# Writing out SyncE's order from branch a on, and moving branch a's gate sigmoids behind each panel's evacuation

## The chip, the core and the metric

The kernel runs on one core of a Trainium2 chip. The core has TensorE (PE; its weight loads are listed apart as PEld), VectorE (DVE), ScalarE (ACT), GpSimd (POOL) and SyncE (SP), which here issues most of the DMAs. Each engine works through its own queue in order; semaphores make one wait for another. The metric is the device time of one execution in microseconds, lower is better.

## The reference

One layer of a hybrid encoder on 1024 prompt rows and 64 sample rows (1088 in all, kept transposed, channels on partitions):

```python
z = xn @ w_in                                  # one wide projection
xa, ga, q, k, v, gb, fl, ma, mb = jnp.split(z, ...)
...                                            # branch a: conv, recurrence; branch b: attention
ya = ya * jax.nn.silu(ga)
yb = yb.reshape(B, L, W_B) * jax.nn.silu(gb)
u = jnp.einsum('bsnw,nwd->bsnd', jnp.stack([ya, yb], axis=2), w_branch)
gates = jax.nn.sigmoid(jnp.stack([ma, mb], axis=2))
mix = jnp.sum(gates * u, axis=2) @ w_o
h = x + rms_norm(mix, g_post)
...
```

The change lies in the lines from `u` to `mix`: sigmoid(ma) * (ya @ w_branch[0]) + sigmoid(mb) * (yb @ w_branch[1]), and the beginning of `@ w_o`.

## The kernel before

All products are float32 in effect, made of three matmuls: each operand is split into a high part (`copy_act`, line 84, on ACT) and a low part (`sub`, line 87, on DVE or POOL), and PE adds high by high (L166), low by high (L167) and high by low (L168).

**Branch a** computes ya @ w_branch[0] in eight panels of 128 output channels (`of` 0 to 7), each of 72 matmuls: 8 input blocks, three column chunks of 368, 368 and 352, three matmuls. Panels 0 and 1 are mostly computed earlier and only finished here (`finish_held`). A panel's raw weights come from DRAM in pairs of panels (`load_panel`, four DMAs of 256 KB on SP, L248); `panel()` takes the next panel, splits the weights of the one behind it (`wh` on ACT, `wl` on DVE) and starts loads when buffers are free. `evac_a` (L1976) multiplies each chunk in PSUM by the gate into a buffer `s`, of which there are two, and L1978 stores it to `d_mix` in DRAM. The gates come as two halves of 544 columns: `half_gate` (L1918) loads one from `d_ma`, `open_gate` (L1922) takes its sigmoid on ACT; there are five such buffers. In panels 3 to 6 `branch_b` also makes the operands of branch b: on POOL yb times its gate, on ACT the high parts `b`, on DVE the low parts and the sums `t`.

**Branch b** computes yb @ w_branch[1] by Strassen's scheme in the form with seven products for two by two blocks: four iterations `i`, each with seven products of 24 matmuls (`product_b`, L2095), on operands `b`, `t0` to `t9` (each split into `t..h` and `t..l` by `split_t`). `put_b` finishes one half panel: two operations on DVE (sum, times the gate), one on POOL (plus branch a's half, `ma_in`, loaded back from `d_mix`), and a store to `d_mx` (L2110). `load_b` fetches the weights of a later iteration. `next_g` and `next_m` issue the loads of the next gate and the next `ma_in`. In the last iteration the raw weights of w_o are loaded (`load_w`, L2056), and `mix_room` (L2082) loads finished panels of `d_mx` back, which `split_mix` splits into `mxh` and `mxl`.

**w_o** starts when branch b's last product is issued: its first 4 input blocks need `wo[0, 0]` and `mix` 0 to 3, the others `wo[0, 1]` (`wqh`, `wql`) and `mix` 4 to 7.

**Order.** A scheduler orders each engine's queue, except within `tc.manual_schedule(engines=...)`: there the named engines keep the order in which the code is written. From branch a's finish to `split_mix(4, 5, 6, 7)` this holds for ACT, DVE and POOL; PE is ordered by the scheduler in both kernels. The panel loads on SP are pinned in program order one by one (`tc.keep_in_program_order`); the rest of SP is the scheduler's.

Of the kernel before, what the change touches and what calls it, by code (L numbers as in the profile page):

```python
# [15 lines left out]
KT = D // P  # L16
# [51 lines left out]
def hybrid_step(tc, a, o):  # L68
# [171 lines left out]
    held_back = [True]  # L240
    n_single = [0]
    ahead = deque()

    def load_panel(dst, src, pin=lambda inst: inst):

        n = KT // 4
        for i in range(4):
            pin(sp.dma_start(dst[:, i * n:(i + 1) * n, :], src[i * n * P:(i + 1) * n * P].rearrange(  # L248
                "(k p) n -> p k n", p=P)))

    def look_ahead():

        while len(ahead) < 2:
            if held_back[0] and len(gates) <= n_gates - PLAIN // 2:
                return
            if not (gates or later):
                return
            src, tags = (gates or later)[0]
            if any(not e[3] and max(len(tags), e[4]) > 1 for e in ahead):
                return  # L260
            (gates or later).popleft()
            if len(tags) > 1:
                dst = raw_pair
                raws_ = panels(raw_pair)
            else:
                dst = raw_half[n_single[0] % 2].rearrange("p (k n) -> p k n", k=KT)
                raws_ = [dst]
                n_single[0] += 1
            load_panel(dst, src, tc.keep_in_program_order)
            for tag, raw in zip(tags, raws_):  # L270
                ahead.append([tag if isinstance(tag, tuple) else ("r", tag), raw, None, False, len(tags)])

# [8 lines left out]
    def panel(eng=None):  # L281

        look_ahead()
        if not ahead:
            return None
        split_next(eng or dve)
        tag, _, w, *_ = ahead.popleft()
        look_ahead()
        split_next(eng or dve)
        look_ahead()  # L290
        return tag, w
# [634 lines left out]
    w = first_w  # L926
    for i in range(len(quads)):
# [10 lines left out]
        w = w_nxt  # L938
# [897 lines left out]
    def finish_held(i, evac):  # L1836
        wh, wl = takes[i][0]["w"]
        for (c, (t0, n)), acc in zip(enumerate(CH), accs["a", i]):
            k = KT - 1
            three(acc[:, :n], wh[:, k, :], wl[:, k, :], ya[k][0][:, t0:t0 + n], ya[k][1][:, t0:t0 + n], False, True)  # L1840
            evac(c, t0, n, acc[:, :n])
# [74 lines left out]
    def half_gate(src, h):  # L1916
        g = p5.tile([P, HT], F32, name="gate", tag="gate", bufs=5)
        sp.dma_start(g[:, :], src[:, H[h]])  # L1918
        return g

    def open_gate(g):
        act.activation(out=g[:, :], in_=g[:, :], func=AF.Sigmoid)  # L1922
        return g

    def gate_in(of):
        return [open_gate(half_gate(d_ma[of], h)) for h in range(2)]

    seq = tc.manual_schedule(engines={act.engine, dve.engine, pool.engine})
    seq.__enter__()
    look_ahead()  # L1930
    split_next(dve, spare)
    fetch(0)
# [30 lines left out]

    w_b = [{} for _ in range(5)]
    g_next = gate_in(0)
    for of in range(KT):
        g = g_next
        if of + 1 < KT:
            g_next = gate_in(of + 1)

        def evac_a(c, t0, n, z, s=None):
            s = s or p5.tile([P, HT], F32, name="s", tag="s", bufs=2)
            for h in range(2):
                a_, b_ = max(t0, h * HT), min(t0 + n, (h + 1) * HT)
                if a_ < b_:
                    dve.tensor_tensor(out=s[:, a_ - t0:b_ - t0], in0=z[:, a_ - t0:b_ - t0],  # L1976
                                      in1=g[h][:, a_ - h * HT:b_ - h * HT], op=ALU.mult)
            sp.dma_start(d_mix[of][:, t0:t0 + n], s[:, :n])  # L1978

        if of < 2:  # L1980
            finish_held(of, evac_a)
        else:
            tag, w = panel()
            assert tag == ("a", of)
            if 3 <= of < 7:
                branch_b(of - 3)
            if of == KT - 2:
                p4.close()
                sp_ = sb("quad_b")
                load_b(0)  # L1990
                splits = split_pair(0, panels(b_raw[0]), w_b[0])
            if of < KT - 1:
                run(panel_steps(mm, *w, ya, evac_a))
            else:
                for _ in range(3):
                    next_g()
                next(splits)
                next(splits)
                wh, wl = w
                mm.close()  # L2000
                psq = ps("psq_b", bufs=4)
                two = [psq.tile([P, 2, 512], F32, name="quad_b") for _ in range(2)]
                accs_ = [two[0][:, 0, :], two[0][:, 1, :], two[1][:, 0, :]]
                ks = (3, 4, 0, 7, 6, 5, 1, 2)
                for k in ks:
                    for c, (t0, n) in enumerate(CH):
                        three(accs_[c][:, :n], wh[:, k, :], wl[:, k, :], ya[k][0][:, t0:t0 + n], ya[k][1][:, t0:t0 + n],
                              k == ks[0], k == ks[-1])
        if of == 2:
            ft_p = mm.tile([P, 512], F32, name="ft_p", tag="acc")  # L2010
            pe.transpose(ft_p[:64, :P], fin.rearrange("p s k -> p (s k)"), ident[:, :])
            ft = p5.tile([P, HT], F32, name="s", tag="s", bufs=2)[:64, :P]
            dve.tensor_copy(ft, ft_p[:64, :P])
            at = 0
            for name, n in (("conv_prompt", 24), ("conv_sample", 24), ("h_prompt", 8), ("h_sample", 8)):
                sp.dma_start(o[name], ft[at:at + n, :])
                at += n
# [83 lines left out]
    def put_b(of, h, z, in1):  # L2101

        g, m = g_got.popleft(), m_got.popleft()
        n_out[0] += 1
        s = (p5.tile([P, HT], F32, name="s", tag="s", bufs=2) if n_out[0] % 3 else late.tile([P, HT], F32, name="s_"))
        s3 = s.rearrange("p (c n) -> p c n", c=2)
        dve.tensor_tensor(out=s3, in0=z, in1=in1, op=ALU.add)
        dve.tensor_tensor(out=s[:, :], in0=s[:, :], in1=g[:, :], op=ALU.mult)
        pool.tensor_tensor(out=s[:, :], in0=s[:, :], in1=m[:, :], op=ALU.add)
        sp.dma_start(d_mx[of][:, H[h]], s[:, :])  # L2110
        next_g()
        next_m()
        open_next()

    def bank():
# [8 lines left out]
    for i in range(4):  # L2124
        w, first, last = w_b[i], i == 0, i == 3
        d1, d2 = 2 * i, 2 * i + 1
        own, splits = splits, iter(()) if last else split_pair(i + 1, panels(b_raw[i + 1]), w_b[i + 1])

        def more():
            next(splits, None)  # L2130

        ta, za = bank()
        product_b(ta, w["a11"], B11, True)
        p1_ = part("p1_")
        copy_act(p1_, za)
        if last:
            raws_ = [load_w(a["w_o"], 0, 0, j) for j in range(2)]
            mix_room(0, "b0", "b2")
            mix_room(1, "b1", "b3")
        td, zd = bank()  # L2140
        product_b(td, w["a12"], B21, True)
        put_b(d1, 0, zd, p1_)
        more()
        if first:
            split_t(8)
            split_t(9)
        else:
            more()
        if last:
            wo[0, 0] = split_w(raws_[0], *small_room())  # L2150
            mix_room(2, "b4", "b6")
            mix_room(3, "b5", "b7")
        elif i + 2 < 4:
            load_b(i + 2)
        tb, zb = bank()
        product_b(tb, w["s2"], T2, True)
        u2 = part("u2_")
        dve.tensor_tensor(out=u2, in0=zb, in1=p1_, op=ALU.add)
        if first:
            next(own)  # L2160
        elif last:
            split_mix(0, 1)
        tcc, zc = bank()
        product_b(tcc, w["s1"], T1, True)
        product_b(tb, w["s3"], T3, False)
        u3 = part("u3_")
        dve.tensor_tensor(out=u3, in0=zb, in1=p1_, op=ALU.add)
        put_b(d2, 1, zc, u3)
        more()
        if last:  # L2170
            split_mix(2, 3)
            mix_room(4, "t0", "t1")
            mix_room(5, "t2", "t3")
        te, ze = bank()
        product_b(te, w["a22"], T4, True)
        put_b(d2, 0, ze, u3)
        more()
        if first:
            more()
        if last:  # L2180
            wo[0, 0] += split_w(raws_[1], *small_room())
        product_b(tcc, w["s4"], B22, False)
        put_b(d1, 1, zc, u2)
        more()
# [289 lines left out]
```

## Time and profile before

| | |
|---|---|
| median of 3 runs | 1443.7 us (1441.4 to 1445.7) |
| profiled execution | 1445.49 us, span on the core 1443.4 us |
| TensorE's granted clock, mean | 0.992 of full speed |
| PE busy | 1409.9 us, 98% of the span |
| DVE, ACT, POOL busy | 910.8, 727.7, 354.7 us |
| moved by DMA | 191.63 MB, mean 133 GB/s |

All times are from the start of the span. Busy times are of an engine; what stands in brackets behind a row is how long the engine had been idle before it and what ended that wait. Branch a's panels 0 to 2 end at 1039.5 us, panel 7 ends at 1113.9, branch b's last product ends at 1206.95, and w_o's first use of `wo[0, 1]` is at 1224.47.

### The profile page before, as it was taken

How to read it: one execution, taken by the hardware profiler on the slowest of the kernel's cores; microseconds unless marked ns; L12 is line 12 of the kernel's file. 1: busy time of each engine (PE TensorE's matmuls, PEld its weight loads, DVE VectorE, ACT ScalarE, POOL GpSimd, SP SyncE). 2: the span in 40 equal slices, each digit the busy share in tenths (PEclk: the TensorE clock that was granted, in tenths of full speed). 3: DMA queues.
4: the chain of work that ended last, by engine and by line, in shares of the span. 5: the costliest groups of instructions: out<-in, count | busy, mean ns of one | idle time of the engine just before them, and what ended most of it. 6: DMA issues, size and time to landing. Idle time of an engine off the chain costs nothing.

```text
span 1443.4 us, 24408 instructions
## 1 busy us (share of the span) xinstructions
PE 1409.9 (98%) x9063; PEld 1335.1 (93%) x9063; DVE 910.8 (63%) x1558; ACT 727.7 (50%) x1338; POOL 354.7 (25%) x430
## 2 busy tenths in 40 slices
PE   9999999999999999999999999999898899999997
PEld 9999999999999999999999899999898898787886
DVE  6646665665662576676766668798456866338544
ACT  5415344344341666666666667878214334324533
POOL 0002332322311444333343400000244454000000
PEclk9999999999999999999999999999999999999999
DMA  5376555655427767556655533421676667224111
GB/s 207 116 131 110 109 176 167 187 169 158 97 74 207 199 142 145 141 136 137 152 137 126 66 67 41 67 41 48 213 233 197 191 200 280 80 73 148 48 47 45
DMA packets 140466, 191.63 MB, mean 133 GB/s; under 512 B 22980, under 2 KB 97772, under 8 KB 140348
## 3 DMA queue, kind: packets, MB, share of 16 engines
q1 hardware_dynamic: 121500, 156.57, 44.1%
q10 hardware_dynamic: 16240, 23.97, 4.6%
q0 software_dynamic: 2608, 9.54, 2.0%
q8 instruction: 71, 1.16, 0.4%
q14 instruction: 47, 0.39, 0.1%
HBM read 127.11 MB, written 62.92 MB: 132 GB/s over the span
## 4 chain that ended last, share of the span: by engine, by line
PE 86%; DMA 5%; DVE 4%; issue 2%; ACT 2%; SPq 1%; DVEq 0%; ACTq 0%; POOL 0%; POOLq 0%
PE quad L810 19%; PE acc L166 12%; PE acc L167 12%; PE acc L168 12%; PE quad_b L2095 5%; PE tp L1193 4%; PE s L1168 2%; PE s L1167 2%; PE pv L1222 2%; PE pv L1220 2%; DMA gate<-d_ma 2%; PE vacc L166 1%; DMA w_raw<-in_w_in 1%; PE vacc L167 1%; PE vacc L168 1%
## 5 line engine op out<-in xcount | busy, mean ns | idle before, releaser
L166 PE MATMUL acc<-xh,wh 128*128 128x368 f32 (+1 forms) x672 | 227.5, 339 | 0.4
L167 PE MATMUL acc<-xl,wh 128*128 128x368 f32 (+1 forms) x672 | 219.8, 327 | 0.0
L168 PE MATMUL acc<-xh,wl 128*128 128x368 f32 (+1 forms) x672 | 219.5, 327 | 0.0
L166 PEld LDWEIGHTS acc<-xh,wh 128*128 128x128 f32 x672 | 126.4, 188 | 1.9 <-DVE nm L1147 1.3
L167 PEld LDWEIGHTS acc<-xl,wh 128*128 128x128 f32 x672 | 126.7, 189 | 0.6
L168 PEld LDWEIGHTS acc<-xh,wl 128*128 128x128 f32 x672 | 126.4, 188 | 0.0
L87 DVE TENSOR_TENSOR wl<-w_raw,wh 128x1024 fp32r<-128x1024 f32 (+1 forms) x67 | 76.8, 1148 | 74.8 <-ACT wh L84 73.1
L84 ACT ACTIVATE th<-tp 128x512 fp32r<-128x512 f32 (+1 forms) x160 | 86.8, 550 | 64.5 <-PE tp L1193 54.1
L87 DVE TENSOR_TENSOR tl<-tp,th 128x512 fp32r<-128x512 f32 (+1 forms) x160 | 99.2, 634 | 29.4 <-ACT th L84 27.8
L1153 POOL TENSOR_SCALAR pb<-pb,sm 128x640 f32<-128x640 f32 (+1 forms) x64 | 61.8, 965 | 166.2 <-DVE sm L1152 155.3
L84 ACT ACTIVATE wh<-w_raw 128x1024 fp32r<-128x1024 f32 (+1 forms) x67 | 62.5, 936 | 76.4 <-PE quad L810 42.7
L810 PE MATMUL quad<-xh,wh 128*128 128x272 f32 x448 | 93.9, 291 | 0.0
L810 PE MATMUL quad<-xl,wh 128*128 128x272 f32 x448 | 92.6, 288 | 0.0
L810 PE MATMUL quad<-xh,wl 128*128 128x272 f32 x448 | 92.5, 288 | 0.0
L84 ACT ACTIVATE wh<-s 128x512 fp32r<-128x512 f32 x54 | 34.1, 631 | 84.0 <-PE quad L810 48.3
L1150 ACT ACTIVATE pb<-pb,nm 128x640 f32<-128x640 f32 (+1 forms) x64 | 63.3, 989 | 24.8 <-DVE nm L1147 17.2
L1220 PE MATMUL pv<-tl,vv 128*128 128x512 f32 x192 | 70.0, 365 | 2.1 <-DVE y L1232 1.3
L810 PEld LDWEIGHTS quad<-xl,wh 128*128 128x128 f32 x448 | 70.6, 188 | 0.0
L810 PEld LDWEIGHTS quad<-xh,wl 128*128 128x128 f32 x448 | 70.4, 188 | 0.0
L810 PEld LDWEIGHTS quad<-xh,wh 128*128 128x128 f32 x448 | 70.2, 188 | 0.2
L1167 PE MATMUL s<-k,q 128*128 128x128 f32 (+2 forms) x192 | 67.4, 358 | 0.0
L1147 DVE CUSTOM_DVE_ANT_0 pb<-s,mask 128x640 f32<-128x640 f32 (+1 forms) x64 | 64.8, 1012 | 3.7 <-PE s L1168 3.5
(702 smaller groups left out, 3958.4 us busy)
## 6 DMA issues: line engine op xcount, KB each, us to landing
w_raw<-in_w_in SPq DMA_DIRECT2D x56, 256.0 KB
q<-d_q SPq DMA_DIRECT2D x48, 256.0 KB
k<-d_k SPq DMA_DIRECT2D x48, 256.0 KB
w_raw<-in_w_in SPq DMA_DIRECT2D x56, 128.0 KB
wraw<-in_w_in SPq DMA_DIRECT2D x24, 256.0 KB
w_raw<-in_w_branch SPq DMA_DIRECT2D x24, 256.0 KB
d_k<-oh ACTq DMA_DIRECT2D x16, 272.0 KB
d_k<-kl SPq DMA_DIRECT2D x16, 272.0 KB
```

The lines of the kernel that those rows point to most:

```text
L84: return act.activation(out=out, in_=in_, func=AF.Copy, scale=scale)
L87: return eng.tensor_tensor(out=out, in0=in0, in1=in1, op=ALU.subtract)
L166: pe.matmul(out, ah, bh, start=start, stop=False)
L167: pe.matmul(out, ah, bl, start=False, stop=False)
L168: pe.matmul(out, al, bh, start=False, stop=stop)
L810: pe.matmul(acc[:, c, :CW], l[:, k, :], r[:, k, c * CW:(c + 1) * CW], start=(first and k == 0 and p == 0), stop=(k == 3 and p == 2), skip_ ...
L1147: at = book("D", now[0] + HOP_PE, per(D_MAX, n), lambda: dve.tensor_tensor_reduce(out=pr[:, :n], in0=s[:, :n], in1=m, scale=-1.0, scalar=- ...
L1150: at = book("A", at, per(A_EXP, n), lambda: act.activation(out=pr[:, :n], in_=pr[:, :n], func=AF.Exp, scale=-1.0, bias=nm, accum_out=sm))
L1153: return free, book("G", at, per(G_NORM, n), lambda: pool.tensor_scalar(out=pr[:, :n], in0=pr[:, :n], scalar1=sm, scalar2=1.0, op0=ALU.mul ...
L1167: pe.matmul(s[:, c0:c0 + w], t["q1"][:, q], t["k1"][:, c0:c0 + w], start=True, stop=False)
L1220: pe.matmul(pv[:, 512 - n:], v, tl[:, c:c + n], start=(j == 0), stop=False)
L2095: pe.matmul(acc[:, c, :CW], l[:, k, :], r[k // 2][:, k % 2, c * CW:(c + 1) * CW], start=(first and k == 0 and p == 0), stop=(k == 3 and p ...
```

## The change

It does five things, all within the region whose order is written out:

1. SP joins the engines whose order is written; the pins on the panel loads are dropped from there on (`pinned.clear()`).
2. `gate_in` only loads; the sigmoids of panel `of + 1` are taken behind the evacuation of panel `of`.
3. In panel 1 (`of == 1`), `panel()` is called ahead of the evacuations instead of in panel 2.
4. In `put_b` the loads of the next gate and the next `ma_in` are written ahead of the store (the first call leaves them out).
5. `load_b(i + 2)` stands behind the iteration's second `put_b` instead of its first.

```diff
+    pinned = [tc.keep_in_program_order]
...
-            load_panel(dst, src, tc.keep_in_program_order)
+            load_panel(dst, src, *pinned)
...
     def gate_in(of):
-        return [open_gate(half_gate(d_ma[of], h)) for h in range(2)]
-
-    seq = tc.manual_schedule(engines={act.engine, dve.engine, pool.engine})
+        return [half_gate(d_ma[of], h) for h in range(2)]
+
+    seq = tc.manual_schedule(engines={act.engine, dve.engine, pool.engine, sp.engine})
     seq.__enter__()
+    pinned.clear()
...
     g_next = gate_in(0)
+    for g in g_next:
+        open_gate(g)
...
-        if of < 2:
+        if of == 0:
             finish_held(of, evac_a)
+        elif of == 1:
+            left_over = []
+            finish_held(of, lambda *args: left_over.append(args))
+            tag, w = panel()
+            for args in left_over:
+                evac_a(*args)
         else:
-            tag, w = panel()
+            if of > 2:
+                tag, w = panel()
...
+        if of + 1 < KT:
+            for g_ in g_next:
+                open_gate(g_)
...
         g, m = g_got.popleft(), m_got.popleft()
+        if n_out[0]:
+            next_g()
+            next_m()
         n_out[0] += 1
...
         sp.dma_start(d_mx[of][:, H[h]], s[:, :])
-        next_g()
-        next_m()
         open_next()
...
-        elif i + 2 < 4:
-            load_b(i + 2)
...
         put_b(d2, 1, zc, u3)
         more()
+        if i + 2 < 4:
+            load_b(i + 2)
```

What it moves, in the order of the queues. On ACT, from the beginning of branch a's finish (`gate` is a sigmoid, `wh` the split of a panel's weights, `b` a split of branch b's operands), before:

```order
L1922 ACTIVATE gate<-gate 128x544 x8
L84 ACTIVATE wh<-w_raw 128x1024
L1922 ACTIVATE gate<-gate 128x544 x2
L84 ACTIVATE wh<-w_raw 128x1024
L84 ACTIVATE b_12543<-yb_in 128x544
L84 ACTIVATE b_12545<-yb_in 128x544
L1922 ACTIVATE gate<-gate 128x544 x2
```

and now:

```order
L1923 ACTIVATE gate<-gate 128x544 x4
L84 ACTIVATE wh<-w_raw 128x1024
L1923 ACTIVATE gate<-gate 128x544 x4
L84 ACTIVATE wh<-w_raw 128x1024
L84 ACTIVATE b_12541<-yb_in 128x544
L84 ACTIVATE b_12543<-yb_in 128x544
```

The split of panel 3's weights had eight sigmoids ahead of it and has four, that of panel 4 had ten and has eight: each later split has two sigmoids (one panel) fewer ahead of it.

On SP at the same place (`gate<-d_ma` a half gate's load, `d_mix<-s` a chunk's store, `w_raw<-in_w_branch` the load of a pair of panels, here 4 and 5), before:

```order
L1918 DMA gate<-d_ma 128x544 x5
L1978 DMA d_mix<-s 128x368
L1918 DMA gate<-d_ma 128x544
L1978 DMA d_mix<-s 128x368
L1978 DMA d_mix<-s 128x352
L1918 DMA gate<-d_ma 128x544
L1978 DMA d_mix<-s 128x368
L1918 DMA gate<-d_ma 128x544
L1978 DMA d_mix<-s 128x368
L1978 DMA d_mix<-s 128x352
L1918 DMA gate<-d_ma 128x544
L248 DMA w_raw<-in_w_branch 128x2x256 x4
```

and now:

```order
L1919 DMA gate<-d_ma 128x544 x4
L1982 DMA d_mix<-s 128x368 x2
L1982 DMA d_mix<-s 128x352
L1919 DMA gate<-d_ma 128x544 x2
L249 DMA w_raw<-in_w_branch 128x2x256 x4
L1982 DMA d_mix<-s 128x368 x2
L1982 DMA d_mix<-s 128x352
```

A panel's three stores stand together and its two gate loads behind them, and the load of the pair stands behind panel 0's stores instead of panel 1's.

On SP at the end of branch b (`d_mx<-s` a half panel's store, `mxl<-d_mx` a finished panel's load, `w_raw<-in_w_o` half of a block of w_o), before:

```order
L2110 DMA d_mx<-s__14127 128x544
L2056 DMA w_raw<-in_w_o 128x2x512
L2110 DMA d_mx<-s 128x544
L2082 DMA mxl_14170<-d_mx 128x1088
L2056 DMA w_raw<-in_w_o 128x2x512
L2082 DMA mxl_14167<-d_mx 128x1088
```

and now:

```order
L2127 DMA d_mx<-s__14127 128x544
L2224 DMA g_post<-in_g_post 128x1024
L2127 DMA d_mx<-s 128x544
L2096 DMA mxl_14167<-d_mx 128x1088
L2096 DMA mxl_14170<-d_mx 128x1088
L2070 DMA w_raw<-in_w_o 128x2x512 x2
```

The two loads for `wo[0, 1]` now stand together, behind the last store and behind the loads of panels 6 and 7. Those for `wo[0, 0]`, which had stood among the stores of the third iteration, likewise stand together now behind the twelfth store (`d_mx<-s__13914`).

## Prediction

> **What bounds the kernel now.** I read the busy table first, then one window for each stage, then the waits of each engine in the stages that the edit touches, then the chain and the timelines. From the page:
>
> ```profile
> span 1443.4 us, 24408 instructions
> PE 1409.9 (98%) x9063; PEld 1335.1 (93%) x9063; DVE 910.8 (63%) x1558; ACT 727.7 (50%) x1338; POOL 354.7 (25%) x430
> ```
>
> TensorE is the bound; only 1443.4 − 1409.9 = 33.5 us of the span can be won without removing a matmul. The windows show how much of it lies here (span of the stage, then busy time of PE, PEld, DVE, ACT, POOL, then PE's granted clock). They are panels 3 to 7 of branch a, and branch b:
>
> ```profile
> 1039.50:1113.90 74.40, 64.35 (x363) 62.33 (x361) 40.83 (x50) 21.10 (x29) 31.71 (x29) 0.93 0.65 206
> 1113.90:1207.00 93.10, 87.70 (x675) 87.09 (x674) 69.32 (x78) 38.28 (x56) 46.05 (x27) 0.96 0.67 220
> ```
>
> PE is idle there for 10.1 and 5.4 us, and both stages have a clock under 1. What they could take is read from PE's timeline: panel 7 runs without a wait, and so does the last product of branch b (12 pairs at 0.25).
>
> ```profile
> 1101.96 0.33 PE L166 MATMUL quad_b<-yah,wh 128*128 128x368 f32 x1
> ...
> 1113.92 0.66 PE L2095 MATMUL quad_b<-b,wh 128*128 128x272 f32 x4
> ...
> 1206.20 0.41 PE L2095 MATMUL quad_b<-t9h,wh 128*128 128x272 f32 x2
> 1206.45 0.41 PE L2095 MATMUL quad_b<-t9l,wh 128*128 128x272 f32 x2
> ```
>
> A panel is 11.96 us, a product 3.0. So panels 3 to 7 lose 74.4 − 5 × 11.96 = 14.6 us, and branch b (28 products) loses 93.1 − 84.0 = 9.1: together 23.7 us. The waits of PE, ACT and DVE in these stages say on whom:
>
> ```profile
> PE acc L166 <- ACT wh L84: 8.3, 2, 4.8
> PE quad_b L2095 <- DVE u__13275 L2158: 3.0, 1, 3.0
> PE quad_b L2095 <- DVE s L1976: 2.4, 1, 2.4
> ACT gate L1922 <- DMA gate<-d_ma: 55.9, 8, 14.5
> DVE s L1976 <- DMA d_mix<-s: 27.5, 9, 6.0
> ```
>
> PE waits 8.3 us for a weight split on ACT, and ACT has stood 55.9 us in front of gate sigmoids whose loads had not landed. The chain of waits shows how the two hang together:
>
> ```profile
> 1077.14 0.99 DVE s L1976 x3
> 1078.13 7.78 DMA gate<-d_ma
> ...
> 1086.57 1.05 ACT wh L84
> ...
> 1095.01 0.96 DVE s L1976 x3
> 1095.98 3.21 DMA gate<-d_ma
> ...
> 1100.94 1.24 DVE wl L87
> ```
>
> It is a ring: DVE's evacuation frees a gate buffer, the next gate half loads into it, its sigmoid stands on ACT ahead of wh, then come wl and branch b's pieces on DVE, and behind these the next evacuation. One turn takes 13 to 18 us (from wl at 1069.77, below, to 1087.6 and 1100.94), and PE wants one every 11.96.
>
> **The change, part by part.**
>
> *Sigmoids behind the evacuation, gate loads in pairs.* No instruction is added or removed. The wh split no longer has the sigmoids that depend on the last evacuation ahead of it, but those of one panel earlier, so the DMA link (7.78, 3.21) leaves the ring. What is late next is DVE itself. Its rows (start, duration, idle before):
>
> ```profile
> 1069.77 1.23 DVE L87 TENSOR_TENSOR wl<-w_raw,wh 128x1024 fp32r<-128x1024 f32 x1 [5.21 <-ACT wh L84]
> ...
> 1073.57 3.65 DVE L87 TENSOR_TENSOR t<-yb_in,t 128x544 f32<-128x544 f32 x1
> 1077.14 1.04 DVE L1976 TENSOR_TENSOR s<-acc,gate 128x368 f32<-128x368 f32 x3
> 1083.64 0.52 DVE L1976 TENSOR_TENSOR s<-acc,gate 128x352 f32<-128x352 f32 x1 [5.47 <-DMA d_mix<-s]
> ...
> 1097.52 0.52 DVE L1976 TENSOR_TENSOR s<-acc,gate 128x352 f32<-128x352 f32 x1 [1.47 <-DMA d_mix<-s]
> ...
> 1104.74 0.73 DVE L87 TENSOR_TENSOR t<-yb_in,t 128x544 f32<-128x544 f32 x1
> ...
> 1121.31 1.04 DVE L1976 TENSOR_TENSOR s<-quad_b,gate 128x368 f32<-128x368 f32 x3
> ```
>
> From one wl to the end of the evacuation behind it DVE needs 1069.77 to 1084.16 = 14.4 us where the store lands late, and, in the next panel (wl at about 1087.65, from the end of the chain's wh at 1087.62), to 1098.04 = 10.4 us. From panel 7's wl to the evacuation of panel 7 it needs 1100.94 to 1121.31 = 20.4 us (t0 to t5 are split in between). Nothing of this is edited. I replay it from panel 3, which PE can now start at 1039.5 and end at 1051.5: the weights of panel 3 are split before panel 1's evacuation and the load of pair 4/5 issues some 10 us earlier. I take wl(4) at 1051.5, when PE ends panel 3 (it needs it then, and panel 2's evacuation, which stands ahead of it on DVE, is over); then wl(5) at 1061.9 (10.4), wl(6) at 1076.3 (14.4, because the load of pair 6/7 again lies in front of the stores), wl(7) at 1086.7 (10.4). PE wants panel 6 at 1075.4, so it waits about 1 us there and nowhere else, and ends panel 7 at about 1100.6. The evacuation of panel 7 comes at 1086.7 + 20.4 = 1107.1, not 1121.31: 14.2 us sooner. It is what branch b's third and later products wait for (the rows of 2.4 and 3.0), so branch b shifts by 14.2. PE is through with panel 7 and two products by 1106.6, so its first gap gets shorter than 2.4, by about 1 us; the second, which hangs on DVE alone, stays, and with it the slow clock behind it:
>
> ```profile
> 1133.40 0.82 PE L2095 MATMUL quad_b<-t4h,wh 128*128 128x272 f32 x2 [3.00 <-DVE u__13275 L2158]
> ...
> 1135.84 0.66 PE L2095 MATMUL quad_b<-t4h,wl 128*128 128x272 f32 x2
> 1136.29 0.46 PE L2095 MATMUL quad_b<-t5h,wh 128*128 128x272 f32 x2
> ```
>
> After the 3.00 us gap a pair took 0.66 instead of 0.41 until 1136.3; this price stays in both kernels. Bounds of the term: if DVE is as slow as 14.4 in both last panels, wl(7) comes at 1090.7 and the gain is 1100.94 − 1090.7 = 10.2; if DVE is never late, panel 7's evacuation follows its end at 1100.8 and the gain is 20.5. Between them I take the replay, **+14.2**.
>
> [...]
>
> *next_g and next_m ahead of the store in put_b.* The gate and mix loads of the next product no longer stand behind a store that waits for POOL. Sigmoids of branch b waited for their loads 1 us in all, so this gains 0; the old order covers it.
>
> *load_b(2), load_b(3) one product later.* They move behind a second store, at 1142.65 for raw 2, whose split ACT begins at 1149.80:
>
> ```profile
> 1142.65 0.32 SPq L2110 DMA_DIRECT2D d_mx<-s  x1
> ...
> 1149.80 1.06 ACT L84 ACTIVATE wh<-w_raw 128x1024 fp32r<-128x1024 f32 x1 [1.59 <-PE quad_b L2095]
> ```
>
> Between them lie 6.8 us for four issues, some 2 us, and a landing of 3.6 to 5.1 (from the rows of w_o below). So the cover is about 1 us or just gone, and the next raw's one iteration later is the same. I take 0; with the cover gone, 0 to 2.
>
> *wo[0,0]'s two loads.* They leave the previous iteration, where the scheduler had put them, and stand behind the twelfth store of branch b. That store, the sum that DVE makes behind wl, and the product of PE that needs its bank:
>
> ```profile
> 1191.79 0.32 SPq L2110 DMA_DIRECT2D d_mx<-s__13914  x1
> ...
> 1195.14 0.72 DVE L2158 TENSOR_TENSOR u__14029<-quad_b,p__13951 128x544 f32<-128x544 f32 x1 [0.22 <-PE quad_b L2095]
> ...
> 1197.94 0.41 PE L2095 MATMUL quad_b<-t4h,wh 128*128 128x272 f32 x2
> ```
>
> Issued at 1192.1 to 1193 and landed 3.6 us later or more, wh and wl (1.05 and 1.24 in the chain's rows) put the end of u (0.72) at about 1199, and behind u stands the bank that PE wants at 1197.94. I take **−1.0**, bounds 0 and −2.6.
>
> *wo[0,1]'s two loads.* Before, the second of them went out at 1211.21 and the first earlier still; now both follow the loads of mxl 6 and 7, which wait for the last store to land. Rows:
>
> ```profile
> 1211.21 1.55 SPq L2056 DMA_DIRECT2D w_raw<-in_w_o  x1
> 1212.87 0.40 SPq L2110 DMA_DIRECT2D d_mx<-s  x1
> ...
> 1217.16 0.32 SPq L2082 DMA_DIRECT2D mxl<-d_mx  x1
> ...
> 1216.37 1.06 ACT L84 ACTIVATE wqh<-w_raw 128x1024 fp32r<-128x1024 f32 x1 [10.46 <-DMA w_raw<-in_w_o]
> 1217.34 2.10 ACT L84 ACTIVATE mxh<-mxl 128x1088 fp32r<-128x1088 f32 x2
> ...
> 1224.47 0.40 PE L166 MATMUL acc<-wqh,mxh 128*128 128x512 f32 x1
> ```
>
> The last mxl went out at 1217.16, so the weight loads go at about 1217.9 and land, with the 3.6 to 5.1 us of the row at 1211.21 (from the issue's end and start to ACT's start at 1216.37), by 1223. Behind them in ACT's order stand both wqh and only then mxh 4 to 7 (1.05 each), with DVE's split behind each: mx 4 is complete at about 1227.8, mx 7 at 1231, where PE wants them at 1224.47 and 1226.6. So PE loses 3.3 to 4.4, and about 1 of slow clock: **−5.0**. Bounds: 3.6 us to land and no slow clock −2.6; 7.6 and a full slow stretch −8.6.
>
> **The sum:** 14.2 − 1.0 − 5.0 = 8.2. The profiled execution took 1445.5 (2.1 over its span); 1445.5 − 8.2 = 1437.3. The median of the runs is 1.8 lower, so I forecast 1443.7 − 8.2 = **1435.5**.
>
> **Rivals.**
> 1. *DVE and the stores set the pace.* DVE's 27.5 us behind store landings are in no part of the ring that is cut; if each of the last panels takes 14.4, the gain is 10.2 − 1.0 − 5.0 = 4.2: 1439.5. For it speaks t<-yb_in,t, 3.65 us where POOL multiplies and 0.73 where it doesn't; against it that only one of the two panels had the late store. [...]
> 2. *The w_o loads are early enough.* [...] Against it: they stand behind mxl 7 on SP.
> 3. *Slower: SP's written order starves panels 6 and 7.* The load of pair 6/7 now stands behind panel 3's three stores and two gate loads, each of which waits in turn. If their wl come no sooner than before (1087.65 and 1100.94), nothing is left of the 14.2, and 1.0 + 5.0 are lost: 1449.7. It decides from wl(6) at 1084.5 on, 8.2 later than in my replay (no gain left), and a loss can be measured 4.3 later. Against it: the load waits for the buffer that wl(5) frees, and that is 8 us sooner (1061.9 for 1069.77).
> 4. *The sigmoids were not the limit:* if wh then waits for something else in its place, only the smaller of PE's two waits for it goes, 8.3 − 4.8 = 3.5, by the earlier load of pair 4/5: 3.5 − 1.0 − 5.0 = −2.5: 1446.2. Against it: gate was 55.9 us of ACT's idle time.
>
> **How the numbers follow.** Forecast 0.48, rival 1 0.20, rival 2 0.18, rival 3 0.08, rival 4 0.06. A change under 0.3% (4.3 us) can't be told from none. Faster than 1439.4: most of the forecast (0.46), rival 2, a third of rival 1, 0.70 in all; within: the rest of rival 1 (0.14), two thirds of rival 4 (0.04) and 0.02 of the forecast, 0.20; slower than 1448.0: rival 3 and the rest of 4, 0.10. Range: the best ends (20.5 − 0 − 2.6 = 17.9) give 1425.8, of which I keep 1427; upward it takes in rival 1 with a costlier w_o (10.2 − 1.0 − 8.6 = 0.6): 1443. Left out are rivals 3 and 4 and the outermost ends.
>
> **What would show it.** Right: ACT's wait before the gate sigmoids falls from 55.9 to under 15, PE's waits for wh vanish, PE waits about 1 us ahead of panel 6, under 2.4 ahead of branch b's third product and still about 3 ahead of its fourth; at w_o a new wait of PE on wqh or mx of 3 to 5 us. Wrong: PE waits 5 us or more at panel 6 for wl or wh (rival 3); DVE's waits for d_mix stores grow past 27.5 (rival 1); no wait at w_o (rival 2). The forecast falls mostly with the pace of DVE's panels, which one late store moves by 4 us.

## Result, and the profile after

Over 20 executions each, the changed kernel takes 1441.8 us (1439.5 to 1445.1) and the kernel before 1444.9 (1441.4 to 1447.3): ratio 0.9981, 95% interval 0.9974 to 0.9988. That is 2 to 4 us faster, less than the 4.3 that the prediction called the least it could tell from none, and well under the 8.2 that it forecast. The profiled execution took 1445.1, the slowest of the twenty, so its profile shows the losses at their largest. Its page begins:

```profile
span 1443.1 us, 24403 instructions
PE 1410.2 (98%) x9063; PEld 1335.3 (93%) x9063; DVE 916.0 (63%) x1558; ACT 728.4 (50%) x1338; POOL 358.1 (25%) x430
```

The windows of the stages, with the same columns as before the change (span, busy time of PE, PEld, DVE, ACT, POOL, PE's granted clock): panels 3 to 7, branch b, w_o up to the first use of `wo[0, 1]`, and the ten microseconds behind it.

```profile
1038.70:1101.20 62.50, 59.83 (x362) 59.52 (x361) 44.09 (x49) 21.32 (x29) 33.72 (x28) 1.00 0.72 246
1101.20:1200.00 98.80, 89.73 (x674) 88.88 (x673) 69.80 (x77) 37.98 (x55) 45.82 (x28) 0.95 0.57 191
1200.00:1220.50 20.50, 16.81 (x74) 13.27 (x72) 6.57 (x8) 3.15 (x4) 5.16 (x11) 1.00 0.76 261
1220.50:1230.50 10.00, 9.36 (x27) 6.76 (x28) 8.59 (x9) 5.70 (x7) 7.08 (x8) 0.66 0.54 169
```

Panels 3 to 7 went from 74.4 to 62.5 us: 11.9 won, and only 2.7 is left above five times 11.96. Of the 11.9, 7.4 is idle time of PE that is gone (10.1 to 2.7) and 4.5 slow clock (PE busy for 59.8 in place of 64.4, granted clock 1.00 for 0.93). Branch b went from 93.1 to 98.8, w_o's first part from 17.5 to 20.5, and the stretch behind it now runs at a clock of 0.66 in the mean, where the ten microseconds behind the same place in the kernel before show 1.00:

```profile
1224.50:1234.50 10.00, 10.00 (x44) 7.93 (x43) 6.40 (x6) 4.69 (x6) 2.92 (x4) 1.00 0.57 177
```

So a gain of 12 us was made where the forecast had it, and in this execution given back in the next 130 us. PE's waits name the places:

```profile
PE quad_b L2109 <- DVE s L1980: 3.1, 1, 3.1
PE quad_b L2109 <- DVE u__14027 L2171: 3.1, 1, 3.1
PE acc L166 <- ACT mxh L84: 2.8, 1, 2.8
PE quad_b L2109 <- DVE u__13267 L2171: 2.7, 1, 2.7
PE quad_b L168 <- DVE wl L87: 2.7, 1, 2.7
```

The waits for wh (8.3 us before) are gone. The first and fourth row are branch b's start, which were there before (2.4 and 3.0). The second and third are new: they are the two places where SP's written order put the loads of w_o behind stores. The fifth, ahead of panel 7, is new too: it is what is left of the ring. The waits of ACT and DVE in the same stages:

```profile
ACT gate L1923 <- DMA gate<-d_ma: 36.1, 7, 11.5
DVE s L1980 <- DMA d_mix<-s: 26.2, 9, 6.3
```

ACT still stands 36 us before gate loads, but PE no longer waits for a wh behind them, and DVE's wait for stores is nearly as long as before (27.5). That the ring is cut shows best in what DVE waited for between the end of panel 2 and the evacuation of panel 7, before and now:

```profile
DVE wl L87 <- ACT wh L84: 17.0, 5, 5.2
...
DVE wl L87 <- ACT wh L84: 0.3, 1, 0.3
```

To compare the kernels below, the table gives the time from the end of panel 2 on PE (`ft_p`, 1039.52 before and 1038.68 after) to the start of some later instruction on PE, and to the span's end, each from one profiled execution.

| kernel | branch b starts | first product on t4 | w_o starts | first use of wo[0, 1] | span's end |
|---|---|---|---|---|---|
| before | 74.4 | 93.9 | 167.4 | 184.9 | 403.9 |
| changed | 62.5 | 82.7 | 161.3 | 181.8 | 404.4 |
| e1, wo[0, 0] early | 61.4 | 81.5 | 153.8 | 175.0 | 396.6 |
| e2, wo[0, 1] early | 65.6 | 83.9 | 161.7 | 179.3 | 398.1 |
| e3, both early | 65.3 | 84.2 | 158.9 | 177.2 | 397.0 |
| e4, sigmoids, SP not written | 62.9 | 82.8 | 155.0 | 172.6 | 391.4 |
| e5, SP written, sigmoids as before | 90.3 | 109.6 | 189.4 | 209.4 | 431.0 |
| e6, POOL's products left out | 60.1 | 80.3 | 156.7 | 177.7 | 400.0 |
| e7, e4 and DVE's order | 64.4 | 79.5 | 153.1 | 170.6 | 389.4 |
| e8, e4 with panel 3's weights late | 63.2 | 83.2 | 157.0 | 174.5 | 393.3 |
| e9, e7 with splits earlier | 63.1 | 79.8 | 153.5 | 171.0 | 390.1 |
| e10, e3 with the order of e9 | 64.1 | 79.2 | 152.8 | 173.0 | 391.8 |

The changed kernel, e1, e2 and e3 have the same code up to the last iterations of branch b, and yet branch b starts 61.4 to 65.6 us behind panel 2: differences of 2 to 4 us in this column are the execution's, not the kernel's.

### The profile page after: what moved, and what is told of

Its sections match the earlier page's. It is cut to its first block, busy times and chain, and to the rows that moved or that the text cites. A ratio compares the mean times of both kernels' runs of the same rounds, so it can differ in the third digit from the quotient of the medians.

```text
span 1443.1 us, 24403 instructions
## 1 busy us (share of the span) xinstructions
PE 1410.2 (98%) x9063; PEld 1335.3 (93%) x9063; DVE 916.0 (63%) x1558; ACT 728.4 (50%) x1338; POOL 358.1 (25%) x430
## 4 chain that ended last, share of the span: by engine, by line
PE 85%; DMA 6%; DVE 5%; issue 2%; ACT 1%; SPq 1%; DVEq 0%; POOL 0%; POOLq 0%; ACTq 0%
PE quad L811 19%; PE acc L166 11%; PE acc L168 11%; PE acc L167 11%; PE quad_b L2109 4%; PE tp L1194 4%; PE s L1169 2%; PE s L1168 2%; PE pv L1223 2%; PE pv L1221 2%; DMA d_mix<-s 2%; PE vacc L166 1%; PE vacc L167 1%; PE vacc L168 1%; DVE wl L87 1%
## 5 line engine op out<-in xcount | busy, mean ns | idle before, releaser
L167 PE MATMUL acc<-xl,wh 128*128 128x368 f32 (+1 forms) x672 | 219.8, 327 | 0.0
L87 DVE TENSOR_TENSOR wl<-w_raw,wh 128x1024 fp32r<-128x1024 f32 (+1 forms) x67 | 79.2, 1183 | 63.6 <-ACT wh L84 41.3
L84 ACT ACTIVATE wh<-w_raw 128x1024 fp32r<-128x1024 f32 (+1 forms) x67 | 62.5, 936 | 84.6 <-PE quad L811 37.5
L811 PE MATMUL quad<-xh,wh 128*128 128x272 f32 x448 | 93.9, 291 | 0.0
L84 ACT ACTIVATE wh<-s 128x512 fp32r<-128x512 f32 x54 | 34.1, 631 | 81.5 <-PE quad L811 47.2
L811 PEld LDWEIGHTS quad<-xl,wh 128*128 128x128 f32 x448 | 70.6, 188 | 0.0
```

The lines of the kernel that those rows point to most:

```text
L84: return act.activation(out=out, in_=in_, func=AF.Copy, scale=scale)
L87: return eng.tensor_tensor(out=out, in0=in0, in1=in1, op=ALU.subtract)
L167: pe.matmul(out, ah, bl, start=False, stop=False)
L811: pe.matmul(acc[:, c, :CW], l[:, k, :], r[:, k, c * CW:(c + 1) * CW], start=(first and k == 0 and p == 0), stop=(k == 3 and p == 2), skip_ ...
```

## Experiments

The theory after the two traces is that branch a's gain is real, and the written order of SP takes it back at two pairs of loads. Its rivals are that DVE's lateness is only carried on from branch a (so that PE would wait whatever SP does), or that the stores and POOL set the pace.

**e1: the loads of wo[0, 0] back in the third iteration.** In the changed kernel, one load goes behind the second `put_b` of that iteration and one behind its third (in code and profile blocks `...` stands for lines left out):

```diff
         if last:
-            raws_ = [load_w(a["w_o"], 0, 0, j) for j in range(2)]
...
+        if i == 2:
+            raws_ = [load_w(a["w_o"], 0, 0, 0)]
...
+        if i == 2:
+            raws_.append(load_w(a["w_o"], 0, 0, 1))
```

> The changed kernel with the two loads of wo[0, 0] issued in the third iteration again, behind the stores of its second and third put_b, instead of behind the twelfth store. Theory (the gain of branch a, some 11 us, is given back at two places, here and at wo[0, 1]): PE's wait ahead of the fourth iteration's product on t4 (3.09 us in the changed kernel) goes, and the slow clock behind it: 3 to 5 us faster than the changed kernel, 6 to 8 faster than before (ratio 0.995). Rival (the wait is DVE's own lateness, carried on from branch a): that wait stays near 3 us and the time is that of the changed kernel, ratio 0.998.

Measured: 1439.7 us, ratio 0.9957 (0.9943 to 0.9971) to before, where the changed kernel has 0.9981: about 3.5 us. From the first product on t4 to the start of w_o it takes 72.2 us where the changed kernel takes 78.6 and the kernel before 73.6; the wait on u in the fourth iteration is gone. Some 1.7 us of the 6.4 between 78.6 and 72.2 can be another thing: in the changed kernel a stretch of half clock (granted clock 0.50 from 1121.96 to 1125.37, 3.4 us, so 1.7 lost) lies right behind the first product on t4, and the author found none there in this execution. Here is what e1 removed, in the changed kernel's timelines of SP, ACT, DVE and PE:

```profile
1179.97 0.32 SPq L2127 DMA_DIRECT2D d_mx<-s__13914  x1
1180.34 1.56 SPq L2070 DMA_DIRECT2D w_raw<-in_w_o  x2
...
1186.37 1.06 ACT L84 ACTIVATE wh<-w_raw 128x1024 fp32r<-128x1024 f32 x1 [7.84 <-DMA w_raw<-in_w_o]
...
1188.60 0.72 DVE L2171 TENSOR_TENSOR u__14027<-quad_b,p__13949 128x544 f32<-128x544 f32 x1
...
1189.37 0.52 PE L2109 MATMUL quad_b<-t4h,wh 128*128 128x272 f32 x2 [3.09 <-DVE u__14027 L2171]
```

The two loads went out at 1180.3 to 1181.9. ACT splits the first of them (`raws_[0]`), whose issue ended at 1180.77, and could begin 5.6 us behind that; wh, wl and u followed as the prediction had it. PE waited 3.09 us, and behind that gap its clock was at half for 3.4 us:

```profile
1189.40:1194.40 5.00, 5.00 (x28) 5.00 (x29) 2.78 (x3) 3.29 (x4) 0.00 (x0) 0.66 0.91 365
```

(a window of 5 us from the end of the wait; a mean clock of 0.66 over it is 3.4 us at half). The theory holds here, and the rival that the lateness comes from branch a falls for this wait, since DVE's order is the same and PE no longer waits.

**e2: the loads of wo[0, 1] early.** In the changed kernel:

```diff
             mix_room(5, "t2", "t3")
+            raws_1 = [load_w(a["w_o"], 0, 1, 0)]
...
             wo[0, 0] += split_w(raws_[1], *small_room())
+            raws_1.append(load_w(a["w_o"], 0, 1, 1))
...
-    wo[0, 1] = room_of(wq, a["w_o"], 0, 1)
+    wo[0, 1] = room_of(wq, a["w_o"], 0, 1, raws_1)
```

With `raws_1` given, `room_of` only splits.

> The changed kernel with the two loads of wo[0, 1] issued as before the change, one behind the loads of mxl 4 and 5 and one ahead of the last store, instead of behind the loads of mxl 6 and 7. Theory: PE's wait for mxh at the first use of wo[0, 1] (2.82 us and 0.62) goes, and 6.8 us of half clock behind it: 3 to 6 us faster than the changed kernel, 6 to 9 faster than before (ratio 0.995). Rival (mxl 6 and 7 themselves come late, since their stores do): a wait on mx of 2 to 3 us stays, at most 1 us faster than the changed kernel.

Measured: 1435.3 us, ratio 0.9930 (0.9918 to 0.9942): 7 us better than the changed kernel, a little more than the theory expected. From w_o's start to the first use of `wo[0, 1]` it takes 17.5 us again, as before the change (20.5 in the changed kernel), and from there to the end 218.8 (222.6, and 218.9 before). What it removed, in the changed kernel:

```profile
1205.93 0.32 SPq L2127 DMA_DIRECT2D d_mx<-s  x1
1210.28 0.80 SPq L2096 DMA_DIRECT2D mxl<-d_mx  x2
1211.12 0.94 SPq L2070 DMA_DIRECT2D w_raw<-in_w_o  x2
...
1217.07 1.06 ACT L84 ACTIVATE wqh<-w_raw 128x1024 fp32r<-128x1024 f32 x1 [19.05 <-DMA w_raw<-in_w_o]
1219.37 4.09 ACT L84 ACTIVATE mxh<-mxl 128x1088 fp32r<-128x1088 f32 x4
...
1220.52 0.50 PE L166 MATMUL acc<-wqh,mxh 128*128 128x512 f32 x1 [2.82 <-ACT mxh L84]
```

The last store goes out at 1205.93, the two mxl loads wait until 1210.28 for it to land, the weight loads stand behind them, and ACT, which keeps its written order, stands idle for 19 us. PE waits 2.82 us, then 0.62, and then runs the next ten microseconds at the mean clock of 0.66 shown in the windows above, 6.8 of them at half. So the stall costs 6.6 us in all, about half of it wait (2.82 and 0.62) and half slow clock (6.8 us at half clock, 3.4 lost).

**e3: both.**

> Both edits of the two other runs together in the changed kernel. Theory: the costs are separate and add up, nothing of branch a's 11 us is given back: 10 to 13 us faster than before (ratio 0.992). Rival (one stall only replaces the other, the lateness is carried through): no faster than the better of the two, ratio 0.995.

Measured: 1435.6 us, ratio 0.9926 (0.9914 to 0.9938), 10 us faster than before. That is the lower end of what the theory expected, but the ratio can't be told from e2's either, which is what the rival said. Within the trace each of the two stalls is gone (t4 to w_o 74.7 us, with half clock right behind the first iteration's gap of 3.41 in it, granted clock 0.60 from 1121.90 to 1128.90; first use of `wo[0, 1]` to the end 219.8), but this execution, like e2's, began branch b at 65.3, some 3 us later than the changed kernel's. Whether the two costs add up is left open by this run; e10 below says more.

**e4: only the sigmoids.** The kernel before with points 2 and 3 of the change; SP stays with the scheduler, `put_b` and `load_b` as before. Against the changed kernel this is the following, and in addition points 4 and 5 taken back:

```diff
-    seq = tc.manual_schedule(engines={act.engine, dve.engine, pool.engine, sp.engine})
+    seq = tc.manual_schedule(engines={act.engine, dve.engine, pool.engine})
     seq.__enter__()
-    pinned.clear()
```

> The kernel before with only the sigmoids moved behind the evacuations and panel 3's weights taken in panel 1; SP stays with the scheduler, put_b and load_b as before. Theory (the ring through the sigmoids is what held branch a, and all that is given back comes from SP's written order): branch a as fast as in the changed kernel, the w_o loads early as before: 9 to 12 us faster than before (ratio 0.993). Rival (the gate loads must be ordered behind the stores as well, SP's written order carries the gain): under 4 us faster, ratio 0.998 or more.

Measured: 1433.8 us, ratio 0.9916 (0.9904 to 0.9929): 12 us faster than before, 9 faster than the change as a whole. All of branch a's gain arrives at the end: 11.6 us at branch b's start, 12.4 at w_o's, 12.5 at the span's end. The longest waits of PE in these stages are:

```profile
PE quad_b L2108 <- DVE s L1979: 2.9, 1, 2.9
PE quad_b L2108 <- DVE u__13275 L2171: 2.0, 1, 2.0
```

The rival, that SP's written order carries the gain, falls.

**e5: only SP written out.** The kernel before with point 1 alone.

```diff
+    pinned = [tc.keep_in_program_order]
...
-            load_panel(dst, src, tc.keep_in_program_order)
+            load_panel(dst, src, *pinned)
...
-    seq = tc.manual_schedule(engines={act.engine, dve.engine, pool.engine})
+    seq = tc.manual_schedule(engines={act.engine, dve.engine, pool.engine, sp.engine})
     seq.__enter__()
+    pinned.clear()
```

> The kernel before with only SP's queue in written order; sigmoids, panel 3's weights, put_b and load_b as before. Theory (the sigmoid move brings branch a's 11 us, SP's written order only costs): PE's waits for wh stay, about 8 us in all, and the loads of w_o come late: 3 to 10 us slower than before (ratio 1.002 to 1.007). Rival (SP's order brings part of the gain, as the gate loads stand in pairs behind the stores): at least as fast as before, ratio under 1.000.

Measured: 1471.0 us, ratio 1.0181 (1.0167 to 1.0195): 26 us slower, where the theory had 3 to 10 and the rival no loss. The theory had the direction and missed the size. The waits of PE and ACT, and then the chain in branch a (start, duration, what):

```profile
PE acc L166 <- ACT wh L84: 17.2, 4, 6.5
ACT gate L1923 <- DMA gate<-d_ma: 76.7, 7, 16.7
```

```profile
1086.94 5.79 DMA d_mix<-s
1092.86 0.54 DVE s L1978
1093.41 0.32 SPq L1980
1093.78 0.42 SPq L1919
...
1094.26 3.43 DMA gate<-d_ma
...
1098.36 1.05 ACT wh L84
```

The written order closes the ring more tightly. The scheduler had put the first gate load between a panel's first and second store; written out, it stands behind the third, and that one waits for the first store to land (5.79 us here), since there are two buffers `s`. With the sigmoids ahead of wh this store landing, the evacuation's last chunk and the gate load all stand in the way of the next panel's weights: branch b starts 15.9 us later than before. The rest, some 11 us, is lost mostly at the same two pairs of loads of w_o as in the changed kernel (t4 to w_o 79.8, w_o to `wo[0, 1]` 20.0). So the parts of the change don't add: the sigmoid move is worth 12 us by itself, and under the written order what stands between e5 and the changed kernel (points 2 to 5) is worth 29 (1471.0 to 1441.8).

**e6: POOL's multiplications left out.** The changed kernel; three of the four products of yb and its gate in a panel are not computed, so yb stays ungated there.

```diff
-            pool.tensor_tensor(out=to, in0=t[:, c], in1=z[:, c], op=ALU.mult)
+            if k >= 4 and c is H[1]:
+                pool.tensor_tensor(out=to, in0=t[:, c], in1=z[:, c], op=ALU.mult)
```

> The changed kernel with three of the four multiplications of yb by its gate left out in each of the panels on POOL (the loads and everything else stay); so yb is not gated. Theory (POOL and DVE block each other for whole instructions, which makes DVE late in panels 4 to 7, where the forecast had it faster): t<-yb_in,t falls from 3.65 to 0.73 us, DVE's turn from wl(6) to wl(7) from 15.2 to 10 to 12, PE's wait of 2.67 us ahead of panel 7 goes, and the evacuation of panel 7 comes 2 to 4 us sooner. Rival (the stores' landing sets the turn): the t rows fall, but DVE waits that much longer for d_mix and the evacuation of panel 7 comes less than 1 us sooner.

Measured: 1439.8 us, ratio 0.9966 (0.9954 to 0.9978), about 2 us under the changed kernel. DVE in the changed kernel, from panel 6's wl on:

```profile
1072.99 1.50 DVE L87 TENSOR_TENSOR wl<-w_raw,wh 128x1024 fp32r<-128x1024 f32 x1
1074.41 1.88 DVE L87 TENSOR_TENSOR t<-yb_in 128x544 f32<-128x544 f32 x1
1076.22 2.51 DVE L87 TENSOR_TENSOR b<-yb_in,b 128x544 fp32r<-128x544 f32 x2
...
1079.40 3.65 DVE L87 TENSOR_TENSOR t<-yb_in,t 128x544 f32<-128x544 f32 x1
...
1087.78 0.52 DVE L1980 TENSOR_TENSOR s<-acc,gate 128x352 f32<-128x352 f32 x1 [3.77 <-DMA d_mix<-s]
1088.22 1.22 DVE L87 TENSOR_TENSOR wl<-w_raw,wh 128x1024 fp32r<-128x1024 f32 x1
...
1109.27 1.05 DVE L1980 TENSOR_TENSOR s<-quad_b,gate 128x368 f32<-128x368 f32 x3
```

and without POOL's products:

```profile
1073.04 1.22 DVE L87 TENSOR_TENSOR wl<-w_raw,wh 128x1024 fp32r<-128x1024 f32 x1
...
1077.99 0.73 DVE L87 TENSOR_TENSOR t<-yb_in,t 128x544 f32<-128x544 f32 x1
...
1084.44 0.53 DVE L1981 TENSOR_TENSOR s<-acc,gate 128x352 f32<-128x352 f32 x1 [4.75 <-DMA d_mix<-s]
1084.88 1.52 DVE L87 TENSOR_TENSOR wl<-w_raw,wh 128x1024 fp32r<-128x1024 f32 x1
...
1106.24 1.04 DVE L1981 TENSOR_TENSOR s<-quad_b,gate 128x368 f32<-128x368 f32 x3
```

The turn from wl to wl falls from 15.2 to 11.8 us, PE's 2.7 us ahead of panel 7 vanishes, and the evacuation of panel 7 comes 68.1 us behind panel 2 in place of 70.6. The theory's figures came, but the rival had a part as well: between 985 and 1240 us DVE's busy time fell from 172.2 to 160.3 us, and its wait for `d_mix` stores rose from 26.2 to 35.6, so of the 11.9 us by which DVE got shorter without POOL's products 9.4 went to waits for the stores, and 2.5 us were left.

**e7: DVE's order at branch b's start.** What e4 left are waits for DVE, which is busy without a break from branch b's first weight split to u2. In e4:

```diff
-    for i in range(6):
+    for i in range(4):
         split_t(i)
     for c, (t0, n) in enumerate(CH):
         evac_a(...)
     next(splits)
+    split_t(4)
+    split_t(5)
...
-        if first:
-            split_t(8)
-            split_t(9)
...
         dve.tensor_tensor(out=u2, in0=zb, in1=p1_, op=ALU.add)
+        if first:
+            split_t(8)
+            split_t(9)
```

> The kernel with only the sigmoids and panel 3's weights moved, and in addition panel 7's evacuation on DVE ahead of the splits t4 and t5 (before: behind them), and u2 of branch b's first iteration ahead of the splits t8 and t9. Theory (what is left after the move is DVE's lateness at two places, PE waits of 2.9 and 2.0 us and the 6.8 us of half clock behind them): both waits shrink, 3 to 6 us faster than that kernel, 15 to 18 faster than before (ratio 0.989). Rival (DVE's total work up to u2 sets the end, its order doesn't matter; or the product on t4 waits for its late split instead): within 1 us of that kernel, ratio 0.9915.

Measured: 1429.8 us, ratio 0.9896 (0.9882 to 0.9909): 15 us faster than before, the lowest of the kernels tried (its interval and e4's overlap a little). The product on t4 starts 79.5 us behind panel 2, 3.3 sooner than in e4. One new wait came, 2.7 us for wl ahead of the product on t2 (the second row; the first is the one ahead of panel 7):

```profile
PE quad_b L168 <- DVE wl L87: 2.8, 1, 2.8
PE quad_b L2110 <- DVE wl L87: 2.7, 1, 2.7
```

**e8: e4 without panel 3's early weights.** Point 2 of the change alone. In e4:

```diff
-        if of == 0:
+        if of < 2:
             finish_held(of, evac_a)
-        elif of == 1:
-            ...
         else:
-            if of > 2:
-                tag, w = panel()
+            tag, w = panel()
```

> The kernel with only the sigmoids moved: panel 3's weights are again split in panel 2, behind panel 1's evacuations. Theory (the two edits take away different waits): PE's wait ahead of panel 3, 3.5 us in the kernel before, stays, but DVE is the later one at panel 7, so most of the gain of 12 stays: 8 to 12 us faster than before (ratio 0.993). Rival (the early weights of panel 3 carry the gain, since they start the following panels' loads 10 us earlier): under 5 us faster, ratio over 0.9965.

Measured: 1432.4 us, ratio 0.9915 (0.9901 to 0.9928), the same as e4. Point 3 brings nothing that can be measured. The theory had the wait ahead of panel 3, 3.5 us in the kernel before, staying without it; it is 1.4.

**e9: the second pair of weight splits ahead of t4 to t7.** In e7:

```diff
     next(splits)
+    next(splits)
     split_t(4)
...
     split_t(7)
-    next(splits)
```

> The kernel with only the sigmoids and panel 3's weights moved and the two moves on DVE at the start of branch b, and in addition the second pair of weight splits ahead of t4 to t7. Theory (PE's 2.7 us wait for wl ahead of the product on t2 is only DVE's order): that wait goes and nothing takes its place: 1 to 3 us faster than without it, ratio 0.988. Rival (t4's split is late next, PE waits as long one product later): the same time, ratio 0.9896.

Measured: 1430.4 us, ratio 0.9900 (0.9884 to 0.9916), no gain over e7. The wait for wl is gone and another stands one product later, as the rival had it:

```profile
PE quad_b L2110 <- DVE u__13271 L2170: 3.5, 1, 3.5
```

Two orders of DVE end at the same time, and from 1098 to 1118 us DVE was busy for 19.34 of 20 us. So DVE's total work up to u2 is most likely the limit at this place; that no third order does better isn't shown.

**e10: SP written out, with the loads early and DVE's order of e9.** The edits of e1, e2 and e9 together in the changed kernel.

> The changed kernel, SP's order written out, with the loads of wo[0, 0] and wo[0, 1] early and the three moves on DVE at the start of branch b. Theory (written order costs only where it puts a load behind a store that is late; with these loads moved nothing is lost by it): within 2 us of the kernel that leaves SP to the scheduler and has the same moves, ratio 0.988 to 0.990. Rival (SP's written order costs more, in branch a's stores and gate loads): 3 us or more slower than that kernel, ratio 0.991 or more.

Measured: 1430.8 us, ratio 0.9903 (0.9888 to 0.9917), the same as e9. So a written order of SP isn't worse in itself: with four loads at other places in it, it comes out level with the scheduler's over the runs, and the way from 0.9981 to 0.9903 is open to it, some of it by DVE's order. As e9 has neither a written SP nor points 4 and 5, those cost nothing here that can be measured either. The profiled execution still shows a small difference: w_o up to the first use of `wo[0, 1]` takes 20.2 us, 17.5 in e9, behind a wait of 2.01 us for wl and slower matmuls behind it (0.63 us each from 1193.97 to 1196.96, 0.39 from 1197.23 on).

## Why the prediction was wrong

It had the mechanism, the places and the sign right, and three terms mis-sized: 8.2 us forecast, about 3 measured (1444.9 − 1441.8). The time lies in its range, near the upper end. In the profiled execution the three terms miss by 3.0, 4.1 and 1.6 us. The steps that failed are the price of the late loads of `wo[0, 0]`, the largest miss, and in the ring the one turn from wl(6) to wl(7). Term by term:

- **The ring, +14.2.** Measured 11.2 at the product on t4 (93.9 to 82.7 us behind panel 2). Panels 3, 4 and 5 went as replayed or better: wl(6) came at 1072.99, 34.3 us behind panel 2's end, where the replay had 36.8. The step that failed is wl(6) to wl(7), 10.4 us taken from the easier of the two rows. It took 15.2, and wl(7) came 2.3 us later than replayed although wl(6) had come 2.5 us sooner; from wl(7) to the evacuation it then took 21.1 us for 20.4. The kernel before has for the same panel, between its wl at 1087.65 and a wait of 1.47 for the store:

```profile
1088.79 0.72 DVE L87 TENSOR_TENSOR t<-yb_in 128x544 f32<-128x544 f32 x1
1089.42 1.35 DVE L87 TENSOR_TENSOR b<-yb_in,b 128x544 fp32r<-128x544 f32 x2
```

Now these took 1.88 and 2.51, which is 2.3 us more, and the wait for the store was 3.77, another 2.3 more. DVE, running earlier, now ran beside POOL's products for more of the panel: a group of POOL's operations (two products and a subtraction) began at 1072.06, beside t and b, where in the kernel before it had begun at 1079.45, in panel 5's turn, while DVE stood waiting for the store. The lower bound, 10.2, was built from a slow turn like this one; taking the dearer row for a panel that moves in time against POOL would have given it, one short of what was measured.
- **wo[0, 0], −1.0.** Measured −5.1: t4 to the start of w_o took 78.6 us for 73.6. This lies outside the bounds (0 to −2.6). Of it, 3.1 is the wait: the load that ACT splits landed 5.6 us behind the end of its issue and not 3.6, for a reason that stays open. Another 1.7 is half clock behind the gap (3.4 us of it), which this term put at nothing without a reason, although the prediction's own rows showed it behind a gap of 3.00. So this is the step of the sum that failed most. e1 confirms that the cost is there: undone, it gives back 3.5 us over the runs.
- **wo[0, 1], −5.0.** Measured −6.6 (2.98 up to the first use, 3.65 behind it); the wait, 3.4, was as expected, the slow clock took 3 to 3.4 us and not 1. e2, which removes it, is 7 us faster than the changed kernel, and so is the largest single cost.
- **put_b and load_b, 0.** No wait of PE appeared in the second and third iteration, and e10, which has these edits, is level with e9, which has not: right.

The sum is 11.2 − 5.1 − 6.6 = −0.5, the span's end of the profiled execution (404.4 for 403.9). The median of the twenty is some 3 us better than this execution; how much of the two stalls the others have can't be seen in times alone.

Rival 1 (DVE and the stores set the pace) is what happened in panel 6: its turn of 14.4 came there, at 15.2. Its sum, 4.2 us faster, was nearest to the measured time, and in part by luck: its ring, 10.2, was close, but it shares the two terms for w_o that came out 5.7 us too small in the profiled execution. Rival 2 fell by e2. Rivals 3 and 4 fell by the first column of the table. What no rival had is e5: that the written order is 26 us slower with the sigmoids in their old place.

Of the signs that were to show it, the waits for wh vanished and PE's waits at w_o came. Three did not come as said: ACT's wait before the gate sigmoids fell to 36.1 us and not under 15, the wait of about 1 us stood ahead of panel 7 and not of panel 6, and was 2.7, and the wait ahead of branch b's third product was 3.09 and not under 2.4. Two readings of the kernel before were also off. PE's busy time holds the slow clock, so 33.5 us of idle time is not all that can be won without removing a matmul: of the 14.6 us that panels 3 to 7 lost, the prediction's own windows have 10.1 as idle. And the first gap of branch b, 2.41 us, had half clock behind it as well as the second: from 1122.9 to 1125.9 a pair of matmuls took 0.66 us or more there (granted clock 0.50 from 1122.70 to 1126.10).

The slow clock did not go by the length of a gap alone: gaps of 2.69, 2.82 and 3.09 us in the changed kernel were each followed by half clock (granted clock 0.50 from 1121.96 to 1125.37, and a mean of 0.66 in the ten and in the five microseconds shown above), and one of 2.73 in e7 was not (1.00). Of POOL and DVE, e6 shows that `t<-yb_in,t` falls from 3.65 to 0.73 us when three of POOL's four products are left out. In the kernel before, DVE's 3.65 from 1073.57 holds two products of POOL, 2.68 from 1073.93; in the changed kernel a product of POOL took 2.33 from 1073.38, beside DVE, and 1.36 from 1085.54, while DVE stood waiting for the store. That each is held up for whole instructions of the other, as the theory of e6 says, is the author's reading of such rows.

## What to carry to other kernels

When a queue's order is written out by hand, look at each load in it whose place the scheduler had chosen, and ask which store or dependent load now stands ahead of it: a load that is free to go early must be written early, and here two pairs of such loads cost as much as the edit had won. Split such a change before keeping it: the sigmoid move was 12 us faster alone, the written order alone 26 slower. And price a short gap of TensorE with the slow clock that may follow it: here 1.7 us behind a wait of 3.09, and 3.4 behind waits of 2.82 and 0.62.

## What was not expected of the hardware

- A stall of PE of about 3 us cost 5 to 7: behind gaps of 3.09 and 2.82 us the clock was at half for 3.4 and 6.8 us (windows at 0.66). In e7 a gap of 2.7 us, ahead of 1115.17, had none behind it (granted clock 1.00 from 1115.20 to 1122.20).
- Two gaps of almost the same length in the changed kernel, 2.67 us ahead of panel 7 (up to 1089.49) and 2.69 ahead of the first product on t4 (up to 1121.38), were paid for differently: behind the first the clock is 1.00, behind the second 0.50 for 3.41 us:

```profile
1091.24:1094.65 3.41, 3.41 (x23) 3.41 (x22) 2.43 (x6) 1.32 (x2) 0.00 (x0) 1.00 1.03 360
...
1121.96:1125.37 3.41, 3.41 (x17) 3.41 (x16) 0.41 (x1) 0.00 (x0) 3.41 (x3) 0.50 0.30 109
```

These rows don't say what made the difference. So such a stall is priced with a range: here from nothing to 3.4 us on top of the gaps.

- The same code in branch a took between 61.4 and 65.6 us from panel 2 to branch b in four profiled kernels that differ only later.
- With three of POOL's four products left out, DVE's work between 985 and 1240 us fell by 11.9 us, and 9.4 of it came back as waits on stores from the two buffers (35.6 us for 26.2); the two limits hide each other.
